# A state space layer: a complex recurrence in 63 serial steps becomes one scan instruction per feature chunk

## The chip, the core and the metric

The kernel runs on one NeuronCore of one Trainium2 chip. The core has five engines that run their own instruction streams: TensorE (PE in the profile, with its weight loads as PEld), VectorE (DVE), ScalarE (ACT), GpSimd (POOL) and SyncE (SP), which here only issues DMAs. ACT and POOL issue DMAs from their own queues too. The metric is the device time of one execution in microseconds (us).

## What is computed

The reference is a chain of two blocks over 512 tokens of 1024 features. The first has a retention and pooling mixer, a mixture of experts (32 experts, the best 4 of them for each token) and a gate with a per-layer embedding. The second has a state space layer (S5), a gated feed-forward layer, a short convolution and one more feed-forward layer. The change is about the state space layer:

```python
def s5_mixer(h, a_re, a_im, log_step, b_re, b_im, c_re, c_im, d, w_out):
    u = h.astype(f32).reshape(bsz, seqlen, SSM_GROUPS, SSM_GROUP)   # 64 groups of 16 features
    dt = jnp.exp(log_step.astype(f32))[:, None]
    mag = jnp.exp(lr * dt)
    abr = mag * jnp.cos(li * dt)          # one complex factor for each group and state (64 states)
    abi = mag * jnp.sin(li * dt)
    ...
    bu_re = jnp.einsum('blgh,gph->blgp', u, bbar_re)
    bu_im = jnp.einsum('blgh,gph->blgp', u, bbar_im)
    _, _, xr, xi = lax.associative_scan(_ssm_combine, (a_r, a_i, bu_re, bu_im), axis=1)
    y = (jnp.einsum('ghp,blgp->blgh', c_re.astype(f32), xr)
         - jnp.einsum('ghp,blgp->blgh', c_im.astype(f32), xi))
    y = y.reshape(bsz, seqlen, D_MODEL) + d.astype(f32) * h.astype(f32)
    y = jax.nn.gelu(y).astype(h.dtype)
    val, gate = jnp.split(y @ w_out, 2, axis=-1)
    return val * jax.nn.sigmoid(gate)
```

Each state obeys x(t) = a x(t-1) + b u(t) with a complex a. All matrix products of the network are done in about fp32 precision, by three products of a high and a low half of each operand.

## The kernel before

Large weights stream from HBM through tiles called raw. ACT makes the high half of each (wh, or eh for the experts, L94), DVE the low half (wl, el, L95), and PE runs three products (L115 to L117). A scheduler orders each engine's instructions when the program is built, by priorities in the code. Work that depends on nothing at hand is fed in between as background steps: the S5 operators from the parameters (S5Prepare, beside the first mixer), and the modulation vectors (ada, L1077).

For each expert the mixture of experts gathers its token rows with an indirect DMA on the POOL queue (xg, L744), turns them on PE (xt, L758), runs the gate and up product (gu) and the down product (dn), and adds its result to the sum in HBM with an indirect DMA on the same queue (acc_d, L750). There are four experts to one table of row numbers (tabim). stage_ple follows, then stage_s5.

stage_s5 cuts the 512 tokens into 64 chunks of 8 and the 1024 features into 8 feature chunks k, of 8 groups each. For each k it normalises and modulates (zh, L1463 on DVE and L1464 on ACT), transposes twice on PE (zt, zu; copied by ACT or DVE to zct and zU), and multiplies by a table made beforehand (s_pt), which gives the contribution of each chunk of tokens to the state (zs, L1493; ACT copies it to zX, L1497). The recurrence over the 63 chunk borders follows, in two generators scan(z) that go side by side, one for the feature chunks 0 to 4 (40 columns of each step) and one for 5 to 7 (24 columns). One step is a multiplication (zr, L1518) and a sum over three terms (L1520) on DVE, and each needs the step before. ACT copies the inputs into zr (L1516) and the finished states into zxq, 16 chunks at a time (L1524). PE then adds the part within a chunk (table T, L1562) and the part from the state before the chunk (table Q, L1573) in zy, and transposes back (zf, L1583); ACT applies GELU (L1586), and the result is split into zgah and zgal for the output product ssm_out (L146, L147 and L115 to L117).

The table Q is made by readout during stage_s5: 16 units of three POOL multiplications of 128x512 (L1117 to L1121, tiles ro), each written to q_d in HBM by SP and read back as zQ. It starts when stage_ple's last normalisation is under way (issue_after(net.rooted)). The steps that the change touches are these lines and S5Prepare's end, where the powers of a are written to e_d.

## Time and profile before

| what | value |
|---|---|
| time, three executions | 2694.13, 2698.68, 2701.28 us (median 2698.68) |
| the profiled execution | 2704.24 us, its span 2701.8 us |
| PE busy | 2558.8 us (95%) |
| DVE busy | 1898.3 us (70%) |
| ACT, POOL busy | 1374.8 us (51%), 430.1 us (16%) |
| HBM traffic | 607.15 MB read, 28.61 MB written |

The span runs from the first to the last instruction that the profiler saw; the rest of the profiled execution's time lies around it. Busy shares are averages over stages with different limits. The stages are, by time: the mixer to about 220 us, router and first gathers to about 300, the experts to 1486, stage_ple to 1566, the S5 layer's part ahead of its output product to 1678, the output product to about 1760, and then the dense layers to the end.

### The profile page before, as it was taken

To read this page: it belongs to the slowest core of one execution; us is meant where nothing else is said; L and a number is where in the kernel's file an instruction comes from. 1 tells how busy PE (TensorE), PEld (TensorE's weight loads), DVE (VectorE), ACT (ScalarE), POOL (GpSimd) and SP (SyncE) were. 2 spreads that over 40 slices of the span, in tenths; PEclk is the share of its full clock that TensorE was granted. 3 is DMA by queue.
4 is the path that set the end of the run, shared out by engine and by line. 5 is a ranking of instruction groups with operands and counts; after the bars stand their busy time and mean duration, and the time that the engine had idled before them with its cause. 6 is when DMAs were issued, how large, how long until landed. Compare 5 with 4: busy or idle time off the path is not lost.

```text
span 2701.8 us, 31654 instructions
## 1 busy us (share of the span) xinstructions
PE 2558.8 (95%) x12270; PEld 1927.6 (71%) x12271; DVE 1898.3 (70%) x2410; ACT 1374.8 (51%) x1513; POOL 430.1 (16%) x252
## 2 busy tenths in 40 slices
PE   8999788999999999999999865999999999999998
PEld 6767555666666666666666755888788888888886
DVE  8974877999999999898988577775553544532333
ACT  7344565777777777777776644242122322322221
POOL 3362312031312112031200071000000000000000
PEclk9999898999999999999999987999999999999999
DMA  6435788999999999999996642754552222223221
GB/s 210 172 110 214 292 289 305 355 341 383 346 383 356 373 360 375 352 358 373 368 372 239 248 150 80 278 188 177 210 214 104 103 97 103 83 86 103 101 85 63
DMA packets 110432, 634.76 MB, mean 235 GB/s; under 512 B 16043, under 2 KB 21419, under 8 KB 43331
## 3 DMA queue, kind: packets, MB, share of 16 engines
q1 hardware_dynamic: 97971, 599.69, 59.6%
q0 software_dynamic: 11584, 28.27, 4.2%
q10 hardware_dynamic: 720, 4.72, 0.4%
q8 instruction: 98, 1.61, 0.2%
q14 instruction: 59, 0.48, 0.1%
HBM read 607.15 MB, written 28.61 MB: 235 GB/s over the span
## 4 chain that ended last, share of the span: by engine, by line
PE 66%; issue 18%; DMA 7%; DVE 6%; POOL 2%; ACT 2%; SPq 0%; POOLq 0%; DVEq 0%; ACTq 0%
PE gu L115 8%; PE gu L116 8%; PE gu L117 8%; PE mm L115 7%; PE mm L116 7%; PE mm L117 7%; PE dn L116 4%; PE dn L117 4%; PE dn L115 4%; DMA xg<-hn_d,tabim 2%; DMA acc_d<-y,tabim 2%; DMA raw<-in_w_ada 1%; PE mm L146 1%; DVE wl L95 1%; PE mm L147 1%
## 5 line engine op out<-in xcount | busy, mean ns | idle before, releaser
L95 DVE TENSOR_TENSOR el<-raw,eh 128x2048 fp32r<-128x2048 f32 (+1 forms) x396 | 874.5, 2221 | 99.3 <-ACT eh L94 93.2
L94 ACT ACTIVATE eh<-raw 128x2048 fp32r<-128x2048 f32 (+1 forms) x396 | 735.2, 1866 | 294.0 <-PE gu L117 209.9
L94 ACT ACTIVATE wh<-raw 128x1024 fp32r<-128x1024 f32 (+1 forms) x238 | 222.0, 981 | 478.2 <-PE mm L116 291.9
L116 PE MATMUL gu<-el,xh 128*88 128x512 f32 x1024 | 404.2, 395 | 0.0
L117 PE MATMUL gu<-eh,xl 128*88 128x512 f32 x1024 | 402.4, 393 | 0.0
L115 PE MATMUL gu<-eh,xh 128*88 128x512 f32 x1024 | 400.6, 397 | 0.0
L95 DVE TENSOR_TENSOR wl<-raw,wh 128x1024 fp32r<-128x1024 f32 (+1 forms) x238 | 265.5, 1148 | 79.9 <-ACT wh L94 79.6
L116 PE MATMUL mm<-nl,wh 128*128 128x512 f32 x816 | 318.3, 390 | 0.0
L115 PE MATMUL mm<-nh,wh 128*128 128x512 f32 x816 | 317.9, 390 | 0.0
L117 PE MATMUL mm<-nh,wl 128*128 128x512 f32 x816 | 316.8, 389 | 0.0
L117 PEld LDWEIGHTS gu<-eh,xl 128*88 128x88 f32 x1024 | 158.4, 155 | 78.4 <-issue 0.5
L116 PEld LDWEIGHTS gu<-el,xh 128*88 128x88 f32 x1024 | 158.9, 155 | 75.8 <-issue 0.5
L115 PEld LDWEIGHTS gu<-eh,xh 128*88 128x88 f32 x1024 | 158.3, 155 | 75.3 <-issue 0.3
L115 PE MATMUL dn<-eh,ath 128*88 128x512 f32 x512 | 204.0, 401 | 0.4
L116 PE MATMUL dn<-el,ath 128*88 128x512 f32 x512 | 202.5, 399 | 0.0
L117 PE MATMUL dn<-eh,atl 128*88 128x512 f32 x512 | 202.4, 396 | 0.0
L750 POOL DMA_INDIRECT acc_d<-y,tabim x32 | 93.8, 2931 | 633.0 <-ACT y L958 566.1
L744 POOL DMA_INDIRECT xg<-hn_d,tabim x32 | 142.2, 4444 | 318.9 <-PE xt L758 157.4
L115 PEld LDWEIGHTS mm<-nh,wh 128*128 128x128 f32 x816 | 153.2, 188 | 32.7
L117 PEld LDWEIGHTS mm<-nh,wl 128*128 128x128 f32 x816 | 153.2, 188 | 32.3
L116 PEld LDWEIGHTS mm<-nl,wh 128*128 128x128 f32 x816 | 153.2, 188 | 31.5
L1681 DVE TENSOR_TENSOR fs<-fs,mm 128x512 f32<-128x512 f32 x44 | 30.2, 687 | 205.8 <-PE mm L117 196.4
(468 smaller groups left out, 3925.7 us busy)
## 6 DMA issues: line engine op xcount, KB each, us to landing
raw<-in_w_gu SPq DMA_DIRECT2D x256, 1024.0 KB, 8.7
raw<-in_w_down SPq DMA_DIRECT2D x128, 1024.0 KB, 7.5
raw<-in_w_ada SPq DMA_DIRECT2D x45, 1024.0 KB, 4.9
raw<-in_w_ffn_in SPq DMA_DIRECT2D x44, 1024.0 KB, 4.8
raw<-in_w_ffn_out SPq DMA_DIRECT2D x32, 704.0 KB, 4.1
raw<-in_conv_in SPq DMA_DIRECT2D x12, 1024.0 KB, 4.9
raw<-in_ssm_out SPq DMA_DIRECT2D x8, 1024.0 KB, 5.0
raw<-in_w_out SPq DMA_DIRECT2D x4, 1024.0 KB, 4.8
```

The lines of the kernel that those rows point to most:

```text
L94: nc.scalar.activation(h, x, AF.Copy)
L95: nc.vector.tensor_tensor(l, x, h.bitcast(F32), ALU.subtract)
L115: mm(ps, sh, mh, start=start, stop=False)
L116: mm(ps, sh, ml, start=False, stop=False)
L117: return mm(ps, sl, mh, start=False, stop=stop).ins
L146: self.nc.tensor.matmul(ps[c], wh, ah, start=k == 0, stop=False)
L147: self.nc.tensor.matmul(ps[c], wl, ah, start=False, stop=False)
L744: return net.nc.gpsimd.indirect_dma_start(out=dst, out_offset=None, in_=net.hn_d[:, :], in_offset=bass.IndirectOffsetOnAxis(ap=idx, axis=0 ...
L750: net.nc.gpsimd.indirect_dma_start(out=net.acc_d[:, :], out_offset=bass.IndirectOffsetOnAxis(ap=idx, axis=0), in_=src, in_offset=None, com ...
L1681: nc.vector.tensor_tensor(t, t, ps, ALU.mult)
```

## The change

The recurrence is rewritten. Instead of multiplying by a complex number at each step, each chunk's contribution is first turned back by the angle that has been passed so far, so that the factor that is left is real; then one instruction (tensor_tensor_scan, line 1568 of the changed kernel) runs all 63 steps for 8 rows of 64 chunk positions at once, with the moduli in zrho; and the result is turned forward again (turned with +1 and -1: one product of 128x512 with the cosines and two of 128x4x64 with the sines, from the table ztab). POOL adds the two products before the scan, and DVE and POOL add two quarters each after it (zxq). This is done for each feature chunk by itself, and the code runs the eight of them as a pipeline: norm, the transposes, states, scan, outputs and to_features follow one another at fixed lags.

The table ztab is new: S5Prepare computes sine and cosine of two sets of 256 angles for each partition (z_d), s5_turns in stage_ple forms their outer products with 24 operations of 128x512 (18 on DVE, 6 on POOL), writes them to r_d over ACT's queue, and stage_s5 loads them (2 x 1 MB).

The read-out (Q) moves from stage_s5 to the experts: 32 units of half the size, one behind each expert's gather, on POOL, with an input fetch and an output write on POOL's own DMA queue. Their inputs are packed in e_d, of which four transfers copy from HBM to HBM in pieces of 128 bytes. Fewer expert weights are fetched ahead (5 for 6 and 8 for 9), the copies to zct are all ACT's, and gal is POOL's for every k, gah ACT's. The part within a chunk (T) is no longer computed ahead, but with the Q part.

```diff
-        moe.prefetch(6)
+        moe.prefetch(5)
...
-        moe.prefetch(9)
+        moe.prefetch(8)
...
         with tc.high_priority(offset=1000):
             nc.scalar.dma_start(bg.bitcast(F32), net.bg_d)
         acts = {}
+        readout = s5_readout(net, pool("s5w", 1))
         def gate_up(e, j):
             gu = []
...
                 if e:
                     self.tables(e + 1)
                     self.fetch(e + 1)
+                    if e:
+                        with tc.issue_after(self.fetched):
+                            next(readout, None)
             with tc.high_priority(offset=0 if e else 1000):
                 a0 = gate_up(e, 0)
             if e:
...
             last = gate_up(e, 1)
             if e == 0:
                 act_fm(e, 0, a0)
+        with tc.issue_after(self.fetched):
+            for _ in readout:
+                pass
         act_fm(NE - 1, 1, last)
         down(NE - 1)
...
+            if b:
+                for h in range(2):
+                    r = slice(64 * h, 64 * h + 64)
+                    nc.vector.tensor_copy(net.turn[r, 0], ar[r, 8, h::2])
+                    nc.vector.tensor_scalar(net.turn[r, 1], ang0[r, h::2], 8.0, None, op0=ALU.mult)
...
+        for j in range(2):
+            o, s, t = temp("ro"), temp("rs"), temp("rk")
+            ang = s[:, :256].rearrange("p (m k) -> p m k", k=8)
+            for k in range(8):
+                nc.vector.tensor_scalar(ang[:, :, k], net.turn[:, 1], float(k * 8 ** j), None, op0=ALU.mult)
+            sincos(net, s[:, :256], o[:, 256:], o[:, :256], s[:, 256:], t[:, :256])
+            nc.sync.dma_start(net.z_d[:, 512 * j:512 * j + 512], o)
+        yield True
...
+            nc.sync.dma_start(net.e_d[:, 16 * h:16 * h + 16, :32], e.rearrange("p (u x) -> p u x", x=32))
+            for j in range(2):
+                x = a[f"s_c{j + 1}"][:, 512 * h:512 * h + 512].rearrange("p (u x) -> p u x", x=32)
+                nc.sync.dma_start(net.e_d[:, 16 * h:16 * h + 16, 32 + 32 * j:64 + 32 * j], x)
...
+def s5_readout(net, pool):
+    gp = net.nc.gpsimd
+    def fetch(q):
+        v = pool.tile([128, 96], F32, tag="c", name=f"ro_c{q}", bufs=2)
+        gp.dma_start(v, net.e_d[:, q])
+        return v
+    v = fetch(0)
+    yield True
+    for q in range(G // 2):
+        er, ei = [v[:, :32].rearrange("p (g r t) -> p r t g", r=2, t=8)[:, r] for r in range(2)]
+        y1, y2 = [v[:, o:o + 32].rearrange("p (g h) -> p g h", h=16) for o in (32, 64)]
+        t = pool.tile([128, 256], F32, tag="t", name=f"ro_t{q}", bufs=2)
+        u = pool.tile([128, 256], F32, tag="u", name=f"ro_u{q}")
+        power_product(gp, t, u, er, ei, y1, y2, ALU.subtract)
+        gp.dma_start(net.q_d[:, q * 256:(q + 1) * 256], t)
+        if q + 1 < G // 2:
+            v = fetch(q + 1)
+        yield True
...
+def s5_turns(net):
+    nc, M = net.nc, 8
+    w = net.op.tile([128, 2048], F32, tag="op", name="tu_w")
+    nc.scalar.dma_start(w[:, :1024], net.z_d)
+    lo, hi = [[w[:, 512 * j + 256 * r:512 * j + 256 * r + 256].rearrange("p (m k) -> p m k", k=8) for r in range(2)]
+              for j in range(2)]
+    sh = [128, M, 8, 8]
+    c = [net.op.tile([128, 2048], F32, tag="op", name=f"tu_c{j}") for j in range(2)]
+    for b in range(4):
+        eng = nc.gpsimd if b == 3 else nc.vector
+        m = slice(M * b, M * b + M)
+        cs = c[b // 2][:, b % 2 * 1024:b % 2 * 1024 + 1024]
+        ov = cs.rearrange("p (m r a b) -> p r m a b", m=M, r=2, a=8)
+        t = w[:, 1024 + 512 * (b == 3):1536 + 512 * (b == 3)].rearrange("p (m a b) -> p m a b", m=M, a=8)
+        x = [v[:, m].unsqueeze(3).to_broadcast(sh) for v in hi]
+        y = [v[:, m].unsqueeze(2).to_broadcast(sh) for v in lo]
+        for r, op in ((0, ALU.subtract), (1, ALU.add)):
+            eng.tensor_tensor(ov[:, r], x[0], y[r], ALU.mult)
+            eng.tensor_tensor(t, x[1], y[1 - r], ALU.mult)
+            eng.tensor_tensor(ov[:, r], ov[:, r], t, op)
+        nc.scalar.dma_start(net.r_d[:, b * 1024:(b + 1) * 1024], cs)
...
-        def scan(z):
-            x = X[z]
-            M = x.shape[3]
-            a8 = net.a8[:, :, 4 * ZK[z]:4 * ZK[z + 1]]
-            xq = XQ[z] = [p1.tile([128, NCH, M], F32, name=f"zxq{z}_{h}") for h in range(2)]
+                        nc.tensor.matmul(pv[64 * h:64 * h + 64, mm, r],
+                                         net.pt[k // 2][:, 8 * (k % 2) + e, 64 * r:64 * r + 64],
+                                         U[k][:, e], start=True, stop=True)
+        def scan(k):
+            pv = sts.pop(k)
+            sh = [128, 4, 2, NCH]
+            o = slice(4 * k, 4 * k + 4)
+            cos, sin = tab[:, o, 0], tab[:, o, 1]
+            ro = rho[k % 2]
+            nc.scalar.copy(ro[:, :, :, 1:], net.turn[:, 0, o].unsqueeze(2).unsqueeze(3).to_broadcast([128, 4, 2, NCH - 1]))
+            def turned(x, sign):
+                w = [p2.tile(sh, F32, tag=f"zw{j}", name=f"zw{k}_{sign}_{j}") for j in range(2)]
+                tt(w[0], x, cos.unsqueeze(2).to_broadcast(sh), ALU.mult)
+                for r in range(2):
+                    if (r == 0) == (sign > 0):
+                        tt(w[1][:, :, r], x[:, :, 1 - r], sin, ALU.mult)
+                    else:
+                        nc.vector.scalar_tensor_tensor(w[1][:, :, r], x[:, :, 1 - r], -1.0, sin, ALU.mult, ALU.mult)
+                return w
+            w = turned(pv, 1)
+            nc.gpsimd.tensor_tensor(w[0], w[0], w[1], ALU.add)
+            x = p2.tile(sh, F32, tag="zx", name=f"zx{k}", bufs=2)
+            flat = "p m r c -> p (m r c)"
+            nc.vector.tensor_tensor_scan(x.rearrange(flat), ro.rearrange(flat), w[0].rearrange(flat), 0.0, ALU.mult, ALU.add)
+            w = turned(x, -1)
+            xq = XQ[k] = p2.tile([128, 2, 4, NCH], F32, tag="zxq", name=f"zxq{k}")
             for h in range(2):
-            done = 0
-            n = S // (6 * M)
-            for c in range(NCH - 1):
-                j = c % n
-                if j == 0:
-                    t = p2.tile([128, S], F32, tag="zh" if z else "t2", name=f"zr{z}_{c}", bufs=4 if z else 3)
-                    t = t[:, :n * 6 * M].rearrange("p (j q m s) -> p j q m s", j=n, q=2, m=M)
-                    e = min(n, NCH - c)
-                    nc.scalar.copy(t[:, :e, :, :, 2], x[:, c:c + e])
-                if c:
-                    nc.vector.tensor_tensor(t[:, j, :, :, :2], a8, x[:, c - 1].rearrange("p r m -> p m r").unsqueeze(1)
-                                            .to_broadcast([128, 2, M, 2]), ALU.mult)
-                    net.scanned = nc.vector.tensor_reduce(x[:, c], t[:, j], AX.X, ALU.add).ins
-                if c % 16 == 15 or c == NCH - 2:
-                    for h in range(2):
-                        for r in range(2):
-                            net.kept = nc.scalar.copy(xq[h][64 * r:64 * r + 64, done + 1:c + 2],
-                                                      x[64 * h:64 * h + 64, done:c + 1, r]).ins
-                    done = c + 1
-                yield True
-        T = {}
+                for r in range(2):
+                    i = slice(64 * h, 64 * h + 64)
+                    (nc.gpsimd if h == r else nc.vector).tensor_tensor(
+                        xq[64 * r:64 * r + 64, h, :, 1:], w[0][i, :, r, :NCH - 1], w[1][i, :, r, :NCH - 1], ALU.add)
...
+            h, l = ga[k]
+            nc.scalar.activation(h, t, AF.Copy)
+            nc.gpsimd.tensor_tensor(l, t, h.bitcast(F32), ALU.subtract)
...
+        for n in range(NK + 6):
+            def stage(f, lag):
+                if 0 <= n - lag < NK:
+                    f(n - lag)
+            stage(norm, 0)
+            stage(to_chunks, 0)
+            stage(to_groups, 1)
+            stage(states, 2)
+            stage(scan, 2)
+            stage(outputs, 4)
+            if n in (5, 7):
+                load_q(n - 1)
+            stage(to_features, 5)
...
-        with tc.tile_pool(name="s5op", bufs=2, reuse_waits="tile") as net.op:
+        with tc.tile_pool(name="s5op", bufs=4, reuse_waits="tile") as net.op:
```

How the instructions stand on three engines, where the names end in numbers of buffers:

DVE in stage_s5 of the kernel before, in the middle of the recurrence (zX holds the states, zr the terms of a step; 13524 and 14068 belong to the first generator, the others to the second):

```order
1635 L1518 TENSOR_TENSOR zr_28_14068<-a_110,zX_13524 128x40x2
1636 L1518 TENSOR_TENSOR zr_14_14102<-a_110,zX_13525 128x24x2
1637 L1520 TENSOR_REDUCE zX_13524<-zr_28_14068 128x40
1638 L1520 TENSOR_REDUCE zX_13525<-zr_14_14102 128x24
1639 L1518 TENSOR_TENSOR zr_28_14068<-a_110,zX_13524 128x40x2
1640 L1518 TENSOR_TENSOR zr_14_14102<-a_110,zX_13525 128x24x2
```

The same place of the changed kernel, from the end of one feature chunk's forward turn to the next one's (zs is in PSUM, L1568 is the scan, zw_1 the turn back and zw_-1 the turn forward):

```order
1605 L1556 TENSOR_TENSOR zw_1_0_14216<-zs_14198,ztab 128x512
1606 L1559 TENSOR_TENSOR zw_1_1_14217<-zs_14198,ztab 128x4x64
1607 L1561 SCALAR_TENSOR_TENSOR zw_1_1_14217<-zs_14198,ztab 128x4x64
1608 L1575 TENSOR_TENSOR zxq_14146<-zw_-1_0_14141,zw_-1_1_14142 64x4x63 x2
1609 L1568 SCALAR_TENSOR_TENSOR zx_14222<-zrho_13872,zw_1_0_14216 128x512
1610 L1556 TENSOR_TENSOR zw_-1_0_14224<-zx_14222,ztab 128x512
1611 L1561 SCALAR_TENSOR_TENSOR zw_-1_1_14225<-zx_14222,ztab 128x4x64
1612 L1559 TENSOR_TENSOR zw_-1_1_14225<-zx_14222,ztab 128x4x64
```

Where 250 short operations stood in one chain, there are now nine longer ones for each feature chunk, and the next chunk's turn back stands ahead of the last chunk's additions.

POOL in stage_s5 of the changed kernel, over two feature chunks (L1565 is the addition ahead of the scan, L1575 the additions behind it, zga the low half of the GELU's result):

```order
419 L1634 TENSOR_TENSOR zga_14486<-zg_14484,zga_14486 128x512
420 L1565 TENSOR_TENSOR zw_1_0_14427<-zw_1_0_14427,zw_1_1_14428 128x512
421 L1634 TENSOR_TENSOR zga_14486<-zg_14573,zga_14486 128x512
422 L1571 MEMSET zxq_14608 128x8
423 L1575 TENSOR_TENSOR zxq_14440<-zw_-1_0_14435,zw_-1_1_14436 64x4x63 x2
424 L1565 TENSOR_TENSOR zw_1_0_14518<-zw_1_0_14518,zw_1_1_14519 128x512
```

The addition that the scan waits for stands behind the last chunk's two additions and one low half on POOL; in the kernel before, POOL had the read-out there.

POOL among the experts before (xg is a gather, acc_d a scatter):

```order
116 L750 DMA acc_d<-y_3793,tabim_2797 600x1024
117 L750 DMA acc_d<-y_4074,tabim_3413 600x1024
118 L750 DMA acc_d<-y_4355,tabim_3413 600x1024
119 L744 DMA xg_2028<-hn_d,tabim_4593 88x1024
120 L744 DMA xg_2030<-hn_d,tabim_4593 88x1024
```

And the same place in the changed kernel (ro_c is the fetched input of a unit, ro_t and ro_u its products):

```order
139 L1441 DMA ro_c_4362<-e_d 128x96
140 L1121 TENSOR_TENSOR ro_t_4356<-ro_t_4356,ro_u_4357 128x256
141 L1452 DMA q_d<-ro_t_4356 128x256
142 L748 DMA acc_d<-y_3876,tabim_2852 600x1024
143 L748 DMA acc_d<-y_4165,tabim_3480 600x1024
144 L748 DMA acc_d<-y_4454,tabim_3480 600x1024
145 L742 DMA xg_2082<-hn_d,tabim_4692 88x1024
146 L1117 TENSOR_TENSOR ro_t_4701<-ro_c_4362 128x256
147 L1119 TENSOR_TENSOR ro_u_4702<-ro_c_4362 128x256
148 L1441 DMA ro_c_4707<-e_d 128x96
149 L742 DMA xg_2084<-hn_d,tabim_4692 88x1024
```

The first gather of a table still stands right behind the scatters, and a unit's operations stand between it and the second gather.

## Rows read from the trace of the kernel before

**Rows 1.** Windows by stage: stretch, length, busy us (instructions) per engine, clock, DMA share, GB/s.

```profile
core 0: us, PE busy (x) PEld busy (x) DVE busy (x) ACT busy (x) POOL busy (x), PEclk, DMA share, GB/s
300.00:1486.00 1186.00, 1153.49 (x5387) 778.46 (x5385) 1052.86 (x855) 837.80 (x638) 238.72 (x65) 0.99 0.95 348
1566.00:1678.00 112.00, 61.36 (x903) 56.73 (x904) 82.82 (x270) 61.48 (x118) 62.80 (x60) 0.76 0.34 120
```

**Rows 2.** Waits of PE from 1566 to 1690: us, times, longest.

```profile
PE zy L1573 <- issue: 46.8, 1, 46.8
```

**Rows 3.** Groups by line, DVE, 1566 to 1655: busy us, mean ns, idle before.

```profile
L1518 DVE TENSOR_TENSOR zr<-a,zX 128x80 f32<-128x80 f32 (+1 forms) x124 | 47.7, 416 | 9.1 <-ACT zX L1497 8.3
L1520 DVE TENSOR_REDUCE zX<-zr 128x40 f32<-128x120 f32 (+1 forms) x124 | 26.5, 247 | 1.5 <-ACT zr L1516 0.5
```

**Rows 4.** Timeline of PE in stage_s5: start, us, instructions in a run.

```profile
1574.40 1.20 PE L1493 MATMUL zs<-zU,s_pt 128*64 128x64 f32 x32
1575.54 1.09 PE L1472 MATMUL zt<-consts,zh 128*64 128x128 f32 x8
1576.55 0.71 PE L1480 MATMUL zu<-consts,zct 64*128 64x64 f32 x8
...
1674.33 3.40 PE L1583 MATMUL zf<-consts,zyt 64*64 64x64 f32 x64
...
1678.07 0.48 PE L146 MATMUL mm<-zgah,wh 128*128 128x512 f32 x1
```

**Rows 5.** Timeline of DVE in stage_ple.

```profile
1503.26 2.36 DVE L95 TENSOR_TENSOR wl<-raw,wh 128x1024 fp32r<-128x1024 f32 x2 [17.57 <-ACT wh L94]
...
1539.03 0.69 DVE L1346 TENSOR_TENSOR res<-res,lg 128x512 f32<-128x512 f32 x1
```

**Rows 6.** Timeline of DVE in stage_s5, as POOL's read-out comes in.

```profile
1586.36 0.24 DVE L1518 TENSOR_TENSOR zr<-a,zX 128x80 f32<-128x80 f32 x1
1586.64 0.28 DVE L1520 TENSOR_REDUCE zX<-zr 128x40 f32<-128x120 f32 x1
...
1591.13 1.02 DVE L1518 TENSOR_TENSOR zr<-a,zX 128x80 f32<-128x80 f32 x1
```

**Rows 7.** Groups by line, POOL, 1566 to 1655.

```profile
L1121 POOL TENSOR_TENSOR ro<-ro 128x512 f32<-128x512 f32 x16 | 20.4, 1275 | 0.7
```

**Rows 8.** Groups by line, PE, 1590 to 1678.

```profile
L1583 PE MATMUL zf<-consts,zyt 64*64 64x64 f32 x256 | 14.4, 221 | 0.0
L1573 PE MATMUL zy<-zQ,zxq 128*64 128x128 f32 x128 | 14.4, 329 | 46.8 <-issue 46.8
L1562 PE MATMUL zy<-zT,zU 128*64 128x128 f32 x128 | 8.5, 279 | 0.0
```

**Rows 9.** Window of four experts, columns as in rows 1.

```profile
585.70:731.05 145.35, 145.24 (x681) 97.63 (x680) 132.61 (x109) 105.67 (x81) 32.09 (x9) 1.00 0.99 362
```

**Rows 10.** Groups by line in that window, DVE and POOL.

```profile
L95 DVE TENSOR_TENSOR el<-raw,eh 128x2048 fp32r<-128x2048 f32 x49 | 111.4, 2286 | 11.7 <-ACT eh L94 10.9
...
L744 POOL DMA_INDIRECT xg<-hn_d,tabim x5 | 33.1, 6612 | 37.3 <-PE xt L758 19.3 <-issue 18.0
```

**Rows 11.** Timelines of POOL, DVE and PE among the experts.

```profile
614.09 1.06 POOL L744 DMA_INDIRECT xg<-hn_d,tabim  x1 [19.31 <-PE xt L758]
...
717.74 3.05 POOL L744 DMA_INDIRECT xg<-hn_d,tabim  x1 [17.06 <-issue]
721.10 12.92 POOL L744 DMA_INDIRECT xg<-hn_d,tabim  x1 [0.30 <-issue]
...
726.37 8.90 DVE L95 TENSOR_TENSOR el<-raw,eh 128x2048 fp32r<-128x2048 f32 x4
...
731.05 0.77 PE L758 MATMUL xt<-consts,xg 88*128 88x88 f32 x8
```

**Rows 12.** Timeline of POOL in stage_ple: a plain DMA's issue.

```profile
1517.86 0.53 POOL L1325 DMA_DIRECT2D half<-in_w_ada  x1 [2.56 <-DVE mods L1080]
```

**Rows 13.** Window ahead of the mixer's end, columns as in rows 1.

```profile
90.00:120.00 30.00, 24.47 (x96) 18.77 (x95) 29.93 (x52) 8.84 (x14) 17.84 (x11) 0.89 0.53 184
```

More of the change, by code (lines that the diff above doesn't have):

```diff
@@ L42 @@
 MORE = 2
-EXTRA = 0
 NA = 5
-ZK = (0, 5, NK)
 class Net:
@@ L1350, in stage_ple @@
         net.pt = []
-        for z in range(2):
-            t = net.op.tile([128, 32, 128], F32, tag="op", name=f"s_pt{z}")
-            for q in range(2):
-                o = slice((2 * z + q) * 2048, (2 * z + q + 1) * 2048)
-                with tc.issue_after(copied[-1]):
-                    nc.scalar.dma_start(t[:, 16 * q:16 * q + 16].rearrange("p g x -> p (g x)"), net.p_d[:, o])
+        for z in range(4):
+            t = net.op.tile([128, 16, 128], F32, tag="op", name=f"s_pt{z}")
+            with tc.issue_after(copied[-1]):
+                nc.scalar.dma_start(t.rearrange("p g x -> p (g x)"), net.p_d[:, z * 2048:(z + 1) * 2048])
             net.pt.append(t)
@@ L1450, in stage_s5 @@
     nc.vector.tensor_tensor(gf, g1, fw, ALU.mult)
-    HG = G // 2
+    tt = nc.vector.tensor_tensor
     with ExitStack() as es:
@@ L1456, in stage_s5 @@
         rb = net.bcast_tok(net.r2)
-        U = [p1.tile([128, HG, NCH], F32, name=f"zU{z}") for z in range(2)]
-        X = [p1.tile([128, NCH, 2, 4 * (ZK[z + 1] - ZK[z])], F32, name=f"zX{z}") for z in range(2)]
-        XQ, hts, cts = {}, {}, {}
+        tab = p1.tile([128, G // 2, 2, NCH], F32, name="ztab")
+        tv = tab.rearrange("p m r c -> p (m r c)")
+        rho = [p1.tile([128, 4, 2, NCH], F32, name=f"zrho{j}") for j in range(2)]
+        for j in range(2):
+            nc.gpsimd.memset(rho[j][:, :, :, 0], 0.0)
+        U, XQ, hts, cts, sts = {}, {}, {}, {}, {}
         def norm(k):
@@ L1531, in load_t @@
+        T, Q, yts = {}, {}, {}
         def load_t(k):
@@ L1587, in to_features @@
                                  AF.Gelu_apprx_tanh)
-            if k < 4:
-                nc.scalar.activation(gah[:, k], t, AF.Copy)
-            else:
-                nc.vector.tensor_copy(gah[:, k], t)
-            (nc.gpsimd if k < 4 else nc.vector).tensor_tensor(gal[:, k], t, gah[:, k].bitcast(F32), ALU.subtract)
+            if k % 2 == 0:
+                g = op.tile([128, 2, 2, S], F32R, tag="op", name=f"zga{k}")
+                ga[k], ga[k + 1] = [(g[:, 0, j], g[:, 1, j]) for j in range(2)]
@@ L1594, in stage_s5 @@
+            h, l = ga[k]
+            nc.scalar.activation(h, t, AF.Copy)
+            nc.gpsimd.tensor_tensor(l, t, h.bitcast(F32), ALU.subtract)
+        for j in range(2):
+            nc.sync.dma_start(tv[:, 2048 * j:2048 * j + 2048], net.r_d[:, 2048 * j:2048 * j + 2048])
         load_t(0)
+        load_q(0)
         load_t(2)
-        with tc.high_priority(offset=-1000), tc.issue_after(net.rooted):
-            readout(net)
-        for k in range(NK):
-            norm(k)
-        scans = []
@@ L1601, in stage_s5 @@
-        LEAD = 20
-        for z in range(2):
-            ks = range(ZK[z], ZK[z + 1])
-            for n in range(len(ks) + 2):
-                if n < len(ks):
-                    to_chunks(ks[n])
-                if 0 <= n - 1 < len(ks):
-                    to_groups(ks[n - 1])
-                if 0 <= n - 2 < len(ks):
-                    states(ks[n - 2])
-            scans.append(scan(z))
-            for _ in range(LEAD if z == 0 else 0):
-                next(scans[0])
-        for _ in range(NCH):
-            for x in scans:
-                next(x, None)
@@ L1617, in stage_s5 @@
[L1617 to L1620 removed]
+        load_q(2)
         load_t(4)
         load_t(6)
[L1623 to L1631 removed]
+        for n in range(NK + 6):
[11 more added lines that the diff above has]
+            stage(to_features, 5)
@@ L1651, in stage_s5 @@
         net.bg = ada(net, 0, p2, range(8, 20), ("ct", "t2"))
-        with tc.issue_after(net.scanned), tc.issue_after(net.kept):
-            net.linear_fm(a["ssm_out"], NK, lambda k: (gah[:, k], gal[:, k]), evac, rate=2)
+        net.linear_fm(a["ssm_out"], NK, lambda k: ga[k], evac, rate=2)
         net.step(99)
```

116 lines of the change are left out of this document (36 added, 80 removed).

## The prediction, written before the changed kernel ran

> **What bounds the kernel now.** I read the windows by stage first. Among the experts PE is busy for 1153 of 1186 us, and in a steady group of four experts for 145.24 of 145.35 us [rows 1, 9]: there PE sets the pace, and nothing gained on another engine moves the end. The stretch from 1566 to 1678 is different: PE works for 61.4 of 112 us, at a granted clock of 0.76 on average, and DVE for 82.8 [rows 1]. The view of waits puts nearly all of that idle time in one place, 46.8 us ahead of the product with Q [rows 2]. The profile names no releaser for it ("issue"). That product needs zxq, which is copied from the recurrence's states, so I looked at what DVE does meanwhile: 248 short operations, 47.7 us of multiplications and 26.5 us of sums, each waiting for the one before [rows 3]. The output product starts at 1678.07, right behind the last transposes zf, which began at 1674.33 [rows 4]. So the S5 layer ahead of 1678 is bound by a serial chain on DVE, and what shortens the chain moves everything behind it.
>
> **The recurrence: what goes and what comes.** The 74.2 us of short operations go [rows 3]. For each of eight feature chunks come these, and I price them by rows:
> - an operation of 128x512 on DVE takes 0.69 us [rows 5]. One of 128x256 I put between this and the 0.24 us of 128x80 [rows 6], by size: 0.24 + 176/432 x 0.45 = 0.42 us. A turn is one of the first and two of the second: 1.53 us, and there are two: 3.06.
> - DVE's two additions on half the partitions, 252 elements each: 2 x 0.42 = 0.84.
> - the scan of 512 elements has no row. It can't be under a plain operation of that size, 0.69. As each element needs the one before, I bound it above by twice that, 1.38, and take 1.2.
> - POOL's addition of 128x512 ahead of the scan: 1.28 [rows 7]. DVE's two additions of the last chunk stand beside it, but with both inputs in SBUF. While POOL's read-out ran, L1518, of the same kind, went from 0.24 to 1.02 us, and the sum L1520 with one input kept its 0.25 on average [rows 3, 6]. So I count the two one after the other.
>
> That makes 3.06 + 0.84 + 1.2 + 1.28 = 6.4 us a chunk. Bounds: if POOL's addition hides DVE's two and the scan costs 0.69, 1.53 + 1.28 + 0.69 + 1.53 = 5.0 us. If POOL's other work for a chunk (two additions of half the length, 0.64 each, and one low half, 1.28) also stands in the chain and the scan takes 1.38, 6.4 + 0.2 + 2.6 = 9.2 us. POOL's two additions run while DVE turns the next chunk back, with one input in PSUM; the low half stands at some places ahead of the addition that the scan waits for. I take 7.0, nearer the middle.
>
> The first states are there at 1574.40 + 1.20 = 1575.6 [rows 4]. Eight chunks of 7.0 end at 1631.6. Four splits of weights (2.36 us for two [rows 5]) now stand among the last two chunks on DVE: 1636.3. Then the last Q part (14.4/8 = 1.8 [rows 8]), one copy on ACT, which I put at DVE's 0.69, and the last transposes (1.8 [rows 8]) follow: 1640.6. PE allows it: it has 61.4 us of work there [rows 1], or for one chunk 1.20 + 1.09 + 0.71 + 1.8 + 1.8 + 1.06 = 7.7 us [rows 4, 8]; from 1566 on it can't be through before 1627. So the output product starts at about 1641 for 1678.07: **-37 us**. With 9.2 us a chunk it starts near 1658 (-20), and with 5.0 it is PE's 1627 that holds (-51).
>
> The read-out that leaves this stretch ran beside the recurrence and gives nothing by itself beyond undoing its pressure on L1518, which is gone with that line.
>
> **The read-out among the experts.** An expert gets three POOL operations of 128x256 (half of 1.28, so 0.64 each) and two DMA issues on POOL's queue. POOL has time: 32.1 of 145 us busy [rows 9]. Three costs can come out of it. First, if DVE stands still for the three operations, that is 1.9 us for an expert, against (145.35 - 132.61)/4 = 3.2 us of idle time that it has [rows 9]; all of it on PE's path would be 31 x 1.9 = 60 us, none is as likely. Second, the queues: 176 KB more for each expert beside the 13.2 MB that 362 GB/s move in 36.3 us [rows 9], 1.3%; if the DMA share of 0.99 were the pace, 31 x 0.5 = 15 us. Third, the queue order: the issue of a gather on POOL took 1.06 us at 614 and 12.92 us at 721, while DVE ran four el in a row (8.90 us from 726.37 on) [rows 11], and 6.6 us on average in that window [rows 10]. The new DMAs can meet the same: between 0.53 us, a plain issue in stage_ple [rows 12], and 12.92. What stands behind them is the gathers of later experts; the shortest margin that I found is 13.3 us (the first rival). I take **+3 us** for the three: the idle times are there, but not always where a stall falls.
>
> The Trainium skill (SBUF — State Buffer, section "Who interferes with whom") says that a DVE instruction with two SBUF inputs contends with a GpSimd instruction that reads SBUF, and that tensor_tensor on DVE was not seen to stall a DMA issued from GpSimd's queue. The first half agrees with L1518 and L1520. By the second half the issues would cost only their lower end and this term would be about nil, 2667 us in all; the gather of 12.92 us beside nothing longer than el speaks against it, and the measurement decides.
>
> **The table in stage_ple and at the start.** 18 products of 128x512 on DVE cost 18 x 0.69 = 12.4 us. DVE stood idle for 17.6 us before the first split there [rows 5], which takes most of them if the angles' table is loaded; some stand between the splits. I take +2, bounds 0 and 12. In S5Prepare some 16 operations of 256 elements and 16 shorter ones come (16 x 0.42 + 16 x 0.24 = 10.6 us), and some copies go, so about 9. DVE is full there: 29.93 of 30 us from 90 to 120, and PE waits for 5.5 us in that window already [rows 13]. I take +3, bounds 0 and 9.
>
> **Sum.** -37 + 3 + 2 + 3 = -29 us. The profiled execution took 2704.24, so 2675.2; it lies 5.6 us above the median of the three runs, against which the change will be seen: **2670 us**.
>
> **Rivals.**
> - **A late gather among the experts (slower).** The first gather of a group of four was issued at 717.74, and PE turned its rows at 731.05, without a wait [rows 11]: 13.3 us for issue and transfer. The new issues stand ahead of it in POOL's queue, behind which the scatters stand, too. If one blocked issue of the mean 6.6 us [rows 10] delays it in each of the seven later groups, PE waits 7 x 6 = 42 us: 2670 - 3 + 42 = 2709. It decides from a delay of about 5 us a group on, where the S5 gain is gone. For it: gathers do get blocked. Against it: POOL stands idle for 17 us before that gather.
> - **POOL and DVE serial in the recurrence.** At 9.2 us a chunk the S5 part gives 20 instead of 37: 2687. For it: the stretched L1518. Against: PE's and ACT's parts overlap in either case, and only some POOL work stands in the chain.
> - **DMA as the pace of the experts.** +15 for +3: 2682. For it: a share of 0.99; against it: PE waits for no weights in the window.
> - That nothing is gained in S5, as the recurrence wasn't the bound, I rule out by the 46.8 us.
>
> **Chances.** My forecast 0.64, with its own range of 2653 to 2686 (S5 gain of 51 to 26, costs of 5 to 13); the late gather 0.17, 2688 to 2737 (3 to 10 us in each of seven groups); the serial pair 0.11; DMA 0.08. Less than 0.3%, about 8 us, can't be told from no change here. The gathers' case is slower in three quarters (0.13) and beside a small part of no change; with the upper ends of the others no change has 0.08, and faster 0.79. Range: 2653 to 2700; about 0.05 lies below it and 0.14 above.
>
> **What would show it.** Right: PE's idle time before the Q products falls from one of 46.8 us to short ones; the S5 stretch ahead of the output product lasts about 75 us instead of 112; the scan line reads near 1.2 us; a group of four experts still takes 145 to 146 us with PE full. Wrong: xt waiting for xg in several groups; el ending the waits of PE; DVE's turns far above 0.7 us, or POOL as the releaser of the scan for most of a chunk; the expert phase beginning late because DVE came later at the start.

## The result, and the profile after

The changed kernel took a median of 2709.41 us (2700.70 to 2720.34, 20 executions) and the kernel before 2695.59 us (2691.32 to 2706.87, 20 executions): ratio 1.0051, 95% interval 1.0038 to 1.0064. **It is slower by 0.5%.** The forecast was 2670 us, and faster. The profiled execution took 2712.78 us, its span 2711.0.

First comes where the time lies, by stage. The table has every kernel of this study; its bounds are the starts of the first xt, the last dn, the first zs and the last zf. One profiled execution of the same program can lie some 9 us beside its median (2704.24 for 2695.59 before), so sums over columns are rougher than a term that rests on a wait.

| kernel | start | experts | stage_ple | S5 ahead of ssm_out | rest | span |
|---|---|---|---|---|---|---|
| before | 285.9 | 1199.9 | 88.7 | 103.1 | 1024.3 | 2701.8 |
| after | 296.0 | 1230.1 | 94.4 | 67.9 | 1022.5 | 2711.0 |
| e1_no_readout | 297.3 | 1202.9 | 95.9 | 70.4 | 1025.3 | 2691.7 |
| e2_compute_only | 294.3 | 1209.9 | 95.7 | 67.8 | 1027.1 | 2694.9 |
| e3_dma_only | 293.3 | 1232.1 | 94.9 | 67.9 | 1028.5 | 2716.7 |
| e4_early_table | 300.0 | 1199.7 | 92.3 | 67.9 | 1027.8 | 2687.7 |
| e5_same_order | 300.7 | 1227.0 | 94.7 | 67.9 | 1028.6 | 2719.1 |
| e6_sync_queue | 294.3 | 1230.8 | 98.1 | 67.9 | 1025.2 | 2716.3 |
| e7_before_early_table | 280.4 | 1198.8 | 88.7 | 102.3 | 1026.1 | 2696.4 |
| e8_turns_last | 282.8 | 1226.2 | 94.5 | 67.9 | 1023.6 | 2695.0 |
| e9_turns_pool_queue | 297.9 | 1226.6 | 93.9 | 67.9 | 1024.9 | 2711.3 |
| e10_three_mends | 283.4 | 1204.4 | 93.8 | 67.9 | 1026.9 | 2676.4 |
| e11_later_table | 282.6 | 1230.5 | 94.6 | 67.9 | 1029.3 | 2704.9 |
| e12_turns_behind_split | 282.4 | 1205.2 | 92.3 | 70.4 | 1028.7 | 2678.9 |

From before to after: start +10.1, experts +30.3, stage_ple +5.8, S5 -35.2, rest -1.8, together +9.2. The gain came as forecast, and more than all of it was given back in the three stages ahead of it. The waits of PE say where (whole span; us in total, times, longest):

```profile
PE xt L756 <- DMA xg<-hn_d,tabim: 48.7, 8, 13.1
PE spt L1274 <- POOL s_pp L1121: 14.9, 1, 14.9
...
PE ht L1329 <- ACT pj L1314: 6.4, 1, 6.4
PE mm L144 <- ACT res L1338: 4.0, 1, 4.0
PE zy L1612 <- POOL zga L1634: 3.4, 1, 3.4
PE gu L114 <- DVE el L93: 2.9, 5, 0.7
PE zy L1612 <- DVE zxq L1575: 2.7, 2, 2.1
```

The one wait of 46.8 us for Q's product [rows 2] is now 3.4 and 2.7. New are spt for s_pp (the start), ht for pj (stage_ple), and el. The kernel before has xt waiting for xg too:

```profile
PE xt L758 <- DMA xg<-hn_d,tabim: 32.8, 4, 12.6
```

Those four waits are all in the first five experts. The changed kernel has eight, 48.7 us, and the four more stand at the first gather of a table: 7.05, 2.35, 0.42 and 5.95 us.

**The S5 stretch.** The window and, from the groups by line of DVE and POOL from 1612 to 1690 (busy us, mean ns, idle before), the scan with its neighbours:

```profile
1612.00:1690.00 78.00, 68.12 (x904) 61.16 (x903) 60.57 (x87) 43.28 (x70) 34.08 (x43) 0.87 0.32 111
```

```profile
L1568 DVE TENSOR_TENSOR_SCAN zx<-zrho,zw 128x512 f32<-128x512 f32 x8 | 9.8, 1221 | 5.6 <-POOL zw L1565 5.5
...
L1556 DVE TENSOR_TENSOR zw<-zs,ztab 128x512 f32<-128x512 f32 x8 | 5.5, 682 | 0.9 <-PE zs L1541 0.9
L1559 DVE TENSOR_TENSOR zw<-zs,ztab 128x256 f32<-128x256 f32 x8 | 3.3, 411 | 0.0
...
L1565 POOL TENSOR_TENSOR zw<-zw,zw 128x512 f32<-128x512 f32 x8 | 10.9, 1364 | 11.1 <-DVE zw L1561 10.8
```

Against [rows 1] PE is busy for 68 of 78 us instead of 61 of 112, at a clock of 0.87 for 0.76. The chain on DVE is no longer alone the bound. The scans start between 1624.6 and 1676.5, so one chunk takes 51.9/7 = 7.4 us.

**A gather that is late.** The timelines of DVE, POOL and PE at the seventh table of rows; each brackets idle time and its releaser:

```profile
1179.11 0.15 DVE L725 TENSOR_TENSOR tabim<-tabfm,sl 88x4 int32<-88x4 f32 x1
1179.17 0.16 DVE L737 TENSOR_REDUCE tabgm<-sl 88x4 f32<-88x12 f32 x1
1179.25 4.48 DVE L93 TENSOR_TENSOR el<-raw,eh 128x2048 fp32r<-128x2048 f32 x2
...
1189.69 0.68 DVE L772 SCALAR_TENSOR_TENSOR act<-gu,up 88x512 f32<-88x512 f32 x1
1190.78 5.42 DVE L93 TENSOR_TENSOR el<-raw,eh 128x2048 fp32r<-128x2048 f32 x2 [0.40 <-ACT eh L92]
...
1180.12 10.63 POOL L742 DMA_INDIRECT xg<-hn_d,tabim  x1 [19.82 <-PE at L756]
1190.79 0.63 POOL L1117 TENSOR_TENSOR ro_t<-ro_c 128x256 f32<-128x256 f32 x1
...
1199.95 1.43 PE L756 MATMUL xt<-consts,xg 88*128 88x88 f32 x8 [5.95 <-DMA xg<-hn_d,tabim]
```

and the same place before:

```profile
1151.52 0.14 DVE L727 TENSOR_TENSOR tabim<-tabfm,sl 88x4 int32<-88x4 f32 x1
1151.59 0.16 DVE L739 TENSOR_REDUCE tabgm<-sl 88x4 f32<-88x12 f32 x1
1152.29 2.29 DVE L95 TENSOR_TENSOR el<-raw,eh 128x2048 fp32r<-128x2048 f32 x1 [0.55 <-ACT eh L94]
...
1152.52 3.04 POOL L744 DMA_INDIRECT xg<-hn_d,tabim  x1 [16.99 <-issue]
```

POOL stood idle for 19.82 us ahead of the gather: nothing of the read-out is in front of it. The gather itself takes 10.63 us to issue instead of 3.04, while DVE runs el and short operations without idle time; its rows then land 9.2 us later (9.3 for the gather at 717.74 in [rows 11], which took 12.3 us from the start of its issue to landing), and PE stands for 5.95. Behind such a wait PE pays once more in clock (window columns as in rows 1):

```profile
604.64:608.86 4.22, 4.21 (x18) 3.40 (x19) 1.57 (x3) 1.39 (x3) 3.61 (x4) 0.50 1.04 328
899.34:905.82 6.48, 6.48 (x23) 4.71 (x24) 6.28 (x5) 3.01 (x5) 6.15 (x5) 0.50 1.03 358
1199.95:1206.19 6.24, 6.24 (x23) 4.60 (x24) 3.38 (x4) 1.39 (x3) 5.60 (x6) 0.50 1.03 300
```

After the waits of 7.05, 2.35 and 5.95 us the granted clock was 0.50, the lower of its two levels, for 4.2, 6.5 and 6.2 us; a matmul of gu then follows the one before after 0.43 us instead of 0.23. After the wait of 0.42 us the clock stayed at 1.00.

**The start and stage_ple.** The first s_pp product on POOL, at 94.6 before, stands at 131.48 now:

```profile
122.37 0.53 POOL L1225 MEMSET s_z<- 128x512 f32 x1 [4.34 <-DMA z_d<-s_ro]
...
131.48 3.22 POOL L1117 TENSOR_TENSOR s_pp<-s_ar,s_bc 128x512 f32<-128x512 f32 x3
```

The memset of s_z stands ahead of it on POOL and waits for the write of the angles' table (z_d), which DVE has to make first. In stage_ple DVE, ACT and PE read:

```profile
1537.02 1.14 DVE L1476 TENSOR_TENSOR tu_c<-tu_w 128x512 f32<-128x512 f32 x1 [10.93 <-DMA tu_w<-z_d]
1538.08 1.55 DVE L1477 TENSOR_TENSOR tu_w<-tu_w 128x512 f32<-128x512 f32 x1
...
1549.67 0.33 ACTq L1479 DMA_DIRECT2D r_d<-tu_c  x1
1550.04 0.58 ACT L1314 COPY pj<-mm 128x512 f32<-128x512 f32 x1 [9.77 <-DVE tu_c L1478]
...
1550.68 1.12 PE L1329 MATMUL ht<-consts,h 128*128 128x128 f32 x4 [6.38 <-ACT pj L1314]
```

The idle time that was to hide the products was spent waiting for their load; they began behind it, some at twice the price (1.55 us for 0.69), and ACT's copy stood behind the write of their result in its own queue.

### The profile page after: what moved, and what is told of

Its sections match the earlier page's. It is cut to its first block, busy times and chain, and to the rows that moved or that the text cites. A ratio compares the mean times of both kernels' runs of the same rounds, so it can differ in the third digit from the quotient of the medians.

```text
span 2711.0 us, 31653 instructions
## 1 busy us (share of the span) xinstructions
PE 2575.3 (95%) x12270; PEld 1937.7 (71%) x12271; DVE 1905.6 (70%) x2274; ACT 1348.2 (50%) x1469; POOL 618.7 (23%) x402
## 5 line engine op out<-in xcount | busy, mean ns | idle before, releaser
L93 DVE TENSOR_TENSOR el<-raw,eh 128x2048 fp32r<-128x2048 f32 (+1 forms) x396 | 889.5, 2266 | 104.0 <-ACT eh L92 102.9
L92 ACT ACTIVATE eh<-raw 128x2048 fp32r<-128x2048 f32 (+1 forms) x396 | 725.0, 1860 | 167.5 <-PE gu L115 117.2
L748 POOL DMA_INDIRECT acc_d<-y,tabim x32 | 74.4, 2326 | 522.0 <-ACT y L952 519.0
```

The source lines that it names most:

```text
L92: nc.scalar.activation(h, x, AF.Copy)
L93: nc.vector.tensor_tensor(l, x, h.bitcast(F32), ALU.subtract)
L748: net.nc.gpsimd.indirect_dma_start(out=net.acc_d[:, :], out_offset=bass.IndirectOffsetOnAxis(ap=idx, axis=0), in_=src, in_offset=None, com ...
```

## The experiments

All ratios are to the kernel before on the same chip, with 95% intervals. Each diff is against the changed kernel if nothing else is said.

**1 to 3. The read-out in its halves.** e1 computes only the last of the 32 units and writes it to all places of Q, e2 has every unit's POOL operations but only one write at the end (with no fetches after the first), e3 the fetches and writes without the operations; each leaves out a part of the work for Q.

```diff
 # e1; e2 has the products in every unit
-        power_product(gp, t, u, er, ei, y1, y2, ALU.subtract)
-        gp.dma_start(net.q_d[:, q * 256:(q + 1) * 256], t)
-        if q + 1 < G // 2:
-            v = fetch(q + 1)
+        if q + 1 == G // 2:
+            power_product(gp, t, u, er, ei, y1, y2, ALU.subtract)
+            gp.dma_start(net.q_d.rearrange("p (n x) -> p n x", x=256), t.unsqueeze(1).to_broadcast([128, G // 2, 256]))
```

```diff
 # e3
-        power_product(gp, t, u, er, ei, y1, y2, ALU.subtract)
-        gp.dma_start(net.q_d[:, q * 256:(q + 1) * 256], t)
+        if q == 0:
+            power_product(gp, t, u, er, ei, y1, y2, ALU.subtract)
+            keep = t
+        gp.dma_start(net.q_d[:, q * 256:(q + 1) * 256], keep)
```

> The changed kernel without the 32 read-out units among the experts: one unit is computed and written to all of Q at the end, so Q holds wrong numbers, but S5 loads as much as before. Theory A (the read-out's POOL operations and POOL DMAs make the first gather of a group of four late, PE waits for it, and its clock falls behind each wait): the time from the first xt to the last dn goes from 1230 us back to about 1200, and the total to about 2680 (0.6% below the kernel before). Rival B (the experts lose by something else of the change, such as the shorter fetch ahead or the later start): it stays near 1230, and the total near 2709.

> The read-out's three POOL operations in every unit, without the fetches and without the writes (one write at the end fills all of Q, with wrong numbers). If the POOL operations are what costs (A1: they and the splits el on DVE hold one another up, and the gather's issue falls into a denser run of el), experts stay at 1225 to 1230 us. If the DMAs on POOL's queue cost (A2), experts come back to about 1200 us.

> The other half: the fetch and the write of every unit on POOL's queue, without the three operations (the same tile is written 32 times, so Q is wrong). A1: experts back to 1200 to 1205 us. A2: they stay at 1225 to 1230.

Measured: e1 2695.92 us, 1.0001 (0.9990 to 1.0012); e2 2694.42, 0.9986 (0.9975 to 0.9996); e3 2720.31, 1.0093 (1.0070 to 1.0116). The DMAs bring the late gathers: the experts take 1232.1 us with the DMAs alone and 1209.9 with the operations alone. In e1 they are back at 1202.9, so the shorter fetch ahead, which e1 keeps, is not the cause; but e1's total missed the 2680 us that was expected. With the operations alone a group of four experts is what it was, 145.28 us for 145.35 [rows 9], PE full:

```profile
1030.98:1176.26 145.28, 145.16 (x681) 97.61 (x680) 134.57 (x109) 105.72 (x81) 60.34 (x21) 1.00 0.98 361
```

Operations do get held on POOL, but nobody waits there. One of e2's took 12.73 us, at the place where [rows 11] has the gather of 12.92:

```profile
1166.03 12.73 POOL L1117 TENSOR_TENSOR ro_t<-ro_c 128x256 f32<-128x256 f32 x1
```

With the DMAs alone PE waits for a first gather 6.17, 5.43, 1.58 and 5.81 us. In e1 and e2 DVE has the order of before at a new table (act, tabim, tabgm, el, up), in e3 that of after (tabim, tabgm, el, el): the DMAs change what the scheduler puts there. The next four runs ask whether that order, POOL's queue, or the time at which the table is made decides.

**4 and 7. The table of rows one expert earlier**, in the changed kernel (e4) and in the kernel before (e7):

```diff
-                    self.tables(e + 1)
+                    if e == 1:
+                        self.tables(2)
                     self.fetch(e + 1)
+                    if e + 2 < NE:
+                        self.tables(e + 2)
```

> The changed kernel with the table of row numbers of each group of four made one expert earlier, so that the first gather of a group can be issued some 36 us sooner; all else is kept, and the outputs are right. A: PE no longer waits for xg at the later groups (7.1, 2.4, 0.4 and 5.9 us in the changed kernel's profile), nor at the first group of four (13.1 us, which the kernel before has too); with the slow clock behind each wait that is 30 to 45 us, so experts about 1190 us and the total 2665 to 2680. B (not the gathers): no change, 2709.

> The kernel before with the table of each group made one expert earlier, as in e4_early_table. It has no read-out among the experts. Its wait of 12.4 us at 439 us goes, with the slow clock behind it: experts 1183 to 1187 us for 1199.8, total 2680 to 2684. The difference of its experts to those of e4_early_table (1199.7) is what the read-out costs when no gather is late: 13 to 16 us if POOL's operations hold up DVE and PE on their own, 0 to 5 if the gathers were all.

Measured: e4 2692.58 us, 0.9984 (0.9973 to 0.9995); e7 2698.57, 1.0001 (0.9987 to 1.0016). In e4 the gather's issue is as long as in the changed kernel, but PE turns its rows 35 us after its end and waits for nothing:

```profile
1121.95 10.62 POOL L742 DMA_INDIRECT xg<-hn_d,tabim  x1 [19.76 <-PE at L756]
...
1167.85 0.77 PE L756 MATMUL xt<-consts,xg 88*128 88x88 f32 x8
```

That shows the path: a held issue costs time only where the table comes late. e4 and e7 have the same experts, 1199.7 and 1198.8 us, with and without the read-out: by itself it costs about 1 us, by one profile of each. Both stayed above what was expected (about 1190, and 1183 to 1187), because the earlier table has its own price: PE waits for el 11.2 us in 11 waits in e4, and a steady group takes 148.0 us (147.5 in e7) for 145.35; the waits for xg at the first experts, which before had, pay for it.

e7 shows one thing more. It has no read-out at all, and still four of its seven first gathers of a group took 10.63 or 10.64 us to issue, beside the same operations on DVE as in the changed kernel at 1180.12:

```profile
1102.00 0.16 DVE L739 TENSOR_REDUCE tabgm<-sl 88x4 f32<-88x12 f32 x1
1102.08 4.48 DVE L95 TENSOR_TENSOR el<-raw,eh 128x2048 fp32r<-128x2048 f32 x2
...
1102.93 10.64 POOL L744 DMA_INDIRECT xg<-hn_d,tabim  x1 [19.79 <-PE at L758]
```

So a long issue does not need the read-out's DMAs.

**5. DVE's order set by hand.** The last operations of a new table are put behind one el of the down product, and the fetch and the unit behind them:

```diff
+        if self.pending and nm == "w_down" and b == 0:
+            p, self.pending = self.pending, None
+            with tc.issue_after(el):
+                p()
+            self.then()
```

> The changed kernel with one thing forced: in each group of four the last step of the row-number table (tabim) waits in the build's order for the first low half of the down weights, so that on DVE one el and then an operation from PSUM (up) follow it, as in the kernel before, and not two el in a row. All POOL operations and POOL DMAs of the read-out stay. Theory O (the order on DVE behind the table decides how long the gather's issue is held): first gathers of groups are issued in about 3 us, PE waits for xg only where the kernel before does (at about 356 and 451 us), the experts take 1203 to 1212 us and the total about 2690. Rival Q (the read-out's DMAs on POOL's queue themselves hold the gathers): no change, experts 1230 us, total 2709.

Measured: 2719.18 us, 1.0071 (1.0047 to 1.0095), experts 1227.0. Three of six first gathers took 2.39 us to issue, the other three still 11.2:

```profile
1185.46 11.22 POOL L744 DMA_INDIRECT xg<-hn_d,tabim  x1 [18.87 <-DVE tabgm L739]
...
1204.11 1.44 PE L758 MATMUL xt<-consts,xg 88*128 88x88 f32 x8 [6.08 <-DMA xg<-hn_d,tabim]
```

The order alone, in this form, does not decide; the 0.55 us that DVE idled ahead of this el in the kernel before did not come back with it. In the three short ones DVE's next operation came 0.05 to 0.55 us later behind the first el than it does in the long ones, where it follows without a gap.

**6. The read-out's DMAs on SP's queue:**

```diff
-        gp.dma_start(v, net.e_d[:, q])
+        net.nc.sync.dma_start(v, net.e_d[:, q])
...
-        gp.dma_start(net.q_d[:, q * 256:(q + 1) * 256], t)
+        net.nc.sync.dma_start(net.q_d[:, q * 256:(q + 1) * 256], t)
```

> The changed kernel with the read-out's fetches and writes on SP's queue in place of POOL's. The build's order on DVE still has two el right behind the table in five of the six later groups. Q: the gathers are free, experts 1203 to 1212 us, total about 2690. O: PE still waits for xg in those groups, experts about 1225 to 1232 us, total 2705 to 2712.

Measured: 2717.20 us, 1.0073 (1.0053 to 1.0094), experts 1230.8. Five of the six first gathers took what they took in the changed kernel, to 0.03 us; the one at 726.85 took 10.64 us for 4.59. Here is the one that stands at 1180.12 there:

```profile
1181.85 10.64 POOL L742 DMA_INDIRECT xg<-hn_d,tabim  x1 [19.78 <-PE at L756]
```

So it is not the DMAs' presence on POOL's queue that holds the issue. The rows land sooner here (3.6 us behind this one), and the waits for xg at the six are down to 2.21, 0.47 and 0.33 us; but on SP the small transfers stand among the weights, and PE waits 11.8 us for eh in dn and 8.1 for el: the experts are no shorter.

**8. The angles' table and the packing of e_d behind the operators** in S5Prepare:

```diff
-        for j in range(2):
-            o, s, t = temp("ro"), temp("rs"), temp("rk")
...
         nc.sync.dma_start(self.c1, a["s_c1"])
...
+        for j in range(2):
+            o, s, t = temp("ro"), temp("rs"), temp("rk")
...
```

> The changed kernel with the sines and cosines of the turn table and the packing of the read-out's input moved behind the S5 operators in S5Prepare, so that POOL's first products (131 us in the changed kernel, 91 us before) are not held by them. Theory S (that place is why the first gather comes 10 us later, with PE's wait of 14.9 us for s_pp): PE's wait for s_pp goes, the first xt comes at 286 to 290 us instead of 296, total 2699 to 2703. Rival (DVE's added work as such, or the 128-byte copies, are what is late): the first xt stays at 294 to 297 us, total 2709.

Measured: 2699.44 us, 1.0003 (0.9991 to 1.0014). The start is 282.8 us for 296.0, spt waits no more, and the first s_pp stands at 95.9. The ten microseconds were the place of the new work ahead of the operators, not its amount.

**9. The turn table's writes on POOL's queue**, so that ACT's copies don't stand behind them:

```diff
-        nc.scalar.dma_start(net.r_d[:, b * 1024:(b + 1) * 1024], cs)
+        nc.gpsimd.dma_start(net.r_d[:, b * 1024:(b + 1) * 1024], cs)
```

> The changed kernel with the turn table's four writes to HBM issued from POOL's queue in place of ACT's. Theory P (in stage_ple ACT stands in its queue for 9.8 us until DVE has made the first block that it is to write, and the copy that PE's transposes wait for stands behind it): PE's wait of 6.4 us for pj goes, the time from the last dn to the first zs falls from 94.5 to 88 to 90 us, total about 2703 to 2705. Rival (DVE's 18 products are late as such, since the angles' table lands 7 us after its load is issued): it stays at 93 to 95, total 2709.

Measured: 2706.13 us, 1.0040 (1.0026 to 1.0055), stage_ple 93.9 for 94.4. The wait for pj went, and another took its place: PE waits 8.0 us for res (4.0 before the edit), whose copy waits for DVE's lhl, behind the products. The stage did not come down to the 88 to 90 us expected.

**10 and 11. Mends together.** e10 is e4, e8 and e9 in one; e11 is e10 with the table later within the expert:

```diff
                 self.prepare(e + 1)
+            if 0 < e < NE - 2:
+                self.tables(e + 2)
```

> Three edits together: the row-number table one expert earlier (e4), the turn table's angles behind the S5 operators (e8) and its writes on POOL's queue (e9). If the three losses are separate, as the stages' times say: first xt at 283 to 287 us, experts 1197 to 1201, stage_ple 88 to 90, S5 68, total 2668 to 2676, which is 0.7 to 1.0% below the kernel before. If the gathers' waits only move (the start decides how the gather meets DVE), experts go back to 1215 or more and the total to 2685.

> As e10_three_mends, but with the next group's table made behind the preparation of the next expert's rows, some half an expert later, still ahead of the place in the changed kernel. With the table one expert early, PE waited twice a group for el (0.7 and 0.9 us) and a group took 147.4 us for 145.3 without any wait for xg. If that comes from the place of the table's work on DVE, the groups come back to 145 to 146 us and the total to 2655 to 2665; if it is the price of any early table, no difference to e10_three_mends.

Measured: e10 **2679.99 us, 0.9944 (0.9931 to 0.9957)**, faster than both kernels, though not at the 2668 to 2676 expected, as stage_ple stayed at 93.8 us and the experts took 1204.4; e11 2707.46, 1.0053 (1.0040 to 1.0066). In e11 the waits for xg are as short as in e10, but el waits take their place (PE, experts):

```profile
PE gu L114 <- DVE el L93: 19.3, 12, 2.1
PE dn L114 <- DVE el L93: 13.8, 12, 1.8
```

Four groups then take 153 to 154.5 us each. DVE is busy for 135 of 148 us in e10's group, and at neither of the two earlier places did the table's operations come without waits for el. The first gathers of e11's groups, with all of the read-out's DMAs about them, took 2.38 to 4.59 us to issue.

**12. The products of the turn table behind the splits** of stage_ple, on top of e10:

```diff
-        s5_turns(net)
+        turns = s5_turns(net)
+        next(turns)
...
+        with tc.issue_after(part):
+            list(turns)
```

> The kernel with the three mends, and the ten products of the turn table put on VectorE's list behind the splits of the read-out stage's weights instead of ahead of them. Theory (in the read-out stage after the experts TensorE waits for ScalarE's piece, which waits for VectorE's split, because the products stand ahead of it; the wait only changed its place when the load's queue was changed): TensorE's wait of about 8 us for the piece goes, the stage takes 88 to 90 us in place of 93.8, as in the kernel before (88.7), and the time is 2674 to 2676 us, a ratio of 0.992 to 0.993. Rival (the stage is longer because the added load and ScalarE's copies stand in it, wherever the products are): the stage stays at 93 to 95 us and the time at 2680, a ratio of 0.9944; or the products, later now, make the first turn of the last stage late by their 5 to 10 us, and the last stage takes 73 to 78 us in place of 67.9.

Measured: 2681.41 us, 0.9938 (0.9926 to 0.9951), which can't be told from e10. stage_ple took 92.3 us, not 88 to 90. The wait for res is halved, and another has come; S5 is 2.5 us longer. PE from 1500 to 1640:

```profile
PE ts L210 <- DVE lacc L218: 4.2, 1, 4.2
PE mm L144 <- ACT res L1343: 4.2, 1, 4.2
```

The rival came nearer, though its ranges were missed as well (93 to 95 for the stage, or 73 to 78 for S5): PE waits 4.2 us for res as it did in the kernel before, and now the norm's sum (lacc) stands behind the products on DVE. At each of the two places tried in this stage, something that PE needs is behind them.

## Why the prediction was wrong

**The S5 stretch: right.** Forecast -37, measured -35. The scan was taken at 1.2 us and reads 1.22; a turn's operations at 0.69 and 0.42, and they read 0.68 and 0.41; DVE's two additions at 0.84 together, and they read 1.7 on average; a chunk at 7.0, and it reads 7.4. PE's idle time fell to short waits. By the Trainium skill (DVE: opcode table, instruction layouts, handler registers and perf-mode slots, section 6) the built-in scan runs at half throughput; 1.22 beside 0.69 for a product of the same size agrees nearly (1.8 times).

**The experts: the step that failed.** The +3 for the read-out there was +30. Of its three costs two were judged rightly: DVE did not lose by POOL's operations (e2), and the queues carry the bytes (e7 against e4). The third, the gather, was the rival of 0.17, and it decided the sign of the result. The size, in the six groups from expert 4 to expert 28, before and after (window columns as in rows 1):

```profile
438.94:1310.11 871.17, 870.72 (x4081) 588.07 (x4082) 788.95 (x638) 629.80 (x478) 181.38 (x48) 1.00 0.98 360
451.07:1348.75 897.68, 878.91 (x4081) 594.48 (x4082) 800.69 (x638) 622.58 (x477) 329.91 (x165) 0.98 0.97 353
```

Of the +26.5 us, 15.8 are PE's waits for the first gather and 3.0 waits for el; the same 4081 matmuls took 8.2 us longer, most of it at the low clock behind three of the waits. The other 4 lie in the first and the last group. The mechanism was not the one I had priced. I had looked for a new DMA in front of the gather, and held the 17 us of idle time against it; POOL was idle indeed, and the gather's own issue was held. Rows 11 had both cases in view, 3.05 us for the first gather of a table and 12.92 for the second, which has slack. What I did not ask is why the first was short, and whether the change would keep it so. The margin of 13.3 us, of which the rows need 9.3 to land, left 4 us for an issue that can take 13.

What sets the length of an issue stays open. The read-out's DMAs bring the long ones into this kernel, on either queue (e3, e6), and POOL's operations don't (e2). But the DMAs are neither needed for a long issue nor enough for one: e7 has none of them and four issues of 10.6 us, e11 has all of them and first gathers of 4.59 us at most. What the length does go with is DVE. In the fourteen traces, each of the 98 first gathers of a group from expert 4 on ended its issue 1.06 us (within 0.13) behind the end of an el, 33 of them behind the first el that ended meanwhile, the others behind a later one. The 23 of them with tabgm, el, el, atl in a row on DVE all took 10.6 us, with the read-out or without. That fits the reading that the DMAs act by changing what stands on DVE at that place. Which el lets the issue go isn't shown: in e5 one order gave both 2.39 and 11.2 us. By the Trainium skill (SBUF — State Buffer, section "Who interferes with whom") tensor_tensor was not seen to stall such DMAs; here issues of 10.63 us that end with an el differ from that, and the measurement decides.

The rival's own figure, 2709, is the measured time almost exactly, and that is chance. It counted 42 us of PE's waits among the experts, behind new DMAs in POOL's queue; the experts lost 30, by another mechanism, and the start and stage_ple lost 11 more than they were given.

**The start and stage_ple: mis-sized.** +3 was +10, above its bound of 9: the operations were counted, not what stands behind them. The S5 operators' tiles waited for the table's write, and PE for the operators; moving the work gave all of it back (e8). For stage_ple, +2 was +5.8, within its bounds: the 17.6 us of cover were there, but 11 went by before the load had landed.

**Beyond the forecast**, e10 shows that the rewritten recurrence is worth about 0.6% if what it brings along is put elsewhere; the earlier table alone gives the kernel before nothing (e7, 1.0001).

## What to carry to other kernels

When work goes into a stage that is full, its cost can be not its length but what it moves: look for the transfer with the smallest margin, ask what sets that margin, and give it more before adding anything. A background step at the start can be as dear as what stands behind it on its engine. Idle time hides new work only if its inputs are there when the idle time begins.

## What the runs showed of the hardware that was not expected

- POOL's operations and issues beside DVE's el stretch by like amounts: in e2 a product of 128x256 took 12.73 us at the place where a gather's issue took 12.92 before, for 0.63 and 1.06 elsewhere. All 98 first gathers named above ended their issue 1.06 us (within 0.13) behind the end of an el.
- After a wait of 2.35 us that ended at 899.34 the granted clock read 0.50 until 905.82; after one of 0.42 us at 1048.02 it stayed at 1.00.
- DVE paid too, in S5: a turn's product on half the columns took 1.49 us once, for 0.42, and its additions behind the scan 0.9 on average for 0.42, both with two inputs in SBUF beside POOL's work; the scan itself kept 1.21 to 1.23 throughout.
